# Attention values of a decoder block made in quarters between the conv blocks of the input projection

## The chip, the cores and the metric

The kernel runs on one core of one Trainium2 chip. The metric is the device time of one execution in microseconds; the time before is the median of 3 runs. The profile and its trace are of one further execution.

## The reference, cut to what matters

One layer of a hybrid decoder with 512 tokens of width 1024, in float32. Only the first half matters here:

```python
p = h @ W_in                      # columns: q | k | v | conv_B | conv_C | conv_u
q, k = rope(rmsnorm(q)), rope(rmsnorm(k))
o    = sliding_window_attention(q, k, v, sinks)   # window 128, blocks of 128 queries
conv = cb * short_conv(cc * cu, conv_w)           # width 3, causal
y    = concat([rmsnorm(o), rmsnorm(conv)]) @ W_out
x    = x + gate1 * y
```

The second half (a product-key expert layer over 16384 experts) takes most of the time and is the same before and after. In the attention a chunk of 128 queries has 8 heads; each head's scores against 128 or 256 keys get a mask, a maximum that takes in the sink, an exponential, a sum and a division, and the result multiplies the values.

## The kernel before, in words

Everything is laid out with features on the partitions and tokens along the free dimension. A product is three float32 matmuls with weights and activations split in a high and a low part: `parts` (line 184) loads 128x1024 weights into `raw`, ScalarE rounds them to `hi` (line 176), VectorE subtracts to `lo` (line 177), and `mm3` (line 197) issues 24 matmuls of 512 columns. `hi` and `lo` have 4 buffers each.

The first half is one Python loop over a string, `PLAN` (line 50), whose steps are written in the order in which their instructions are to be issued (loop from line 481). A step's letter says what it does:

- `Cmp`: conv block m, part p (`conv`, line 438): one `mm3` of 24 matmuls into a PSUM bank `pj`; part 0 is copied by ScalarE to `cc` (line 442), part 1 becomes the conv `y` on VectorE (lines 446 to 450), part 2 multiplies `y` into `convT` (line 452).
- `An`: scores of chunk n (`attend1`, line 374): 8 matmuls into four banks `sc`; VectorE takes them out into `s`, scaled and masked (line 388, 8 instructions), then the maximum (line 391) and its negative `nm` (line 394); ScalarE takes 8 exponentials (line 397) and a small one for the sink, `es_` (line 401); VectorE divides (line 405).
- `Bn`: values of chunk n (`attend2`, line 408): for each of 4 pairs of heads, TensorE transposes the probabilities into banks `pT` (line 416), ScalarE takes each head's bank out to `pT` in SBUF (line 418), and TensorE multiplies by the values into one bank `po` (line 425), one pair behind the transposes. ScalarE takes `po` out to `attnT` (line 434).
- `M`: two weight columns of the adaLN modulation as dot products on VectorE (`ada`, line 204, line 213); their DMA waits for the last `mm3` issued before.
- `S`, `N`: sums of squares of the conv output (line 236, matmul `ssc` line 237), and its RMSNorm (`part_norm`, line 463).

After the plan come the sums of squares of the attention output (`ssa`), and the output projection (`py`).

The Tile scheduler takes instructions in the order written as priority and settles, when the kernel is built, one fixed order for each engine; each engine then runs its instructions in that order and waits on semaphores. All of `sc`, `pT`, `po`, `pj` and the sums come from one pool of 6 PSUM banks (`bank`, line 110). In the plan before, the four steps `C30 C22 C31 C32` follow each other without attention work between them, and `B2` and `B3` stand behind them with only `S` and `N` between.

Of the kernel before, what the change touches and what calls it, by code (L numbers as in the profile page):

```python
# [19 lines left out]
T = 512  # L20
# [26 lines left out]

PLAN = ("q0 q1 k P2 M r0 V R P3 r1 q2 C00 r2 q3 T C01 M r3 M C02 A0 C10 M C11 A1 M C12 B0 C20 M M M A2 C21 B1 A3 "  # L50
        "C30 M C22 C31 C32 S B2 N B3 M M M")

SM = {}
_o = 0
# [35 lines left out]
def body(tc, p):  # L90
# [19 lines left out]
    def bank(name):  # L110
        return psm.tile([P, 512], F32, tag="m", name=name)
# [122 lines left out]
    def square(ps, b, i, n, w=None):  # L234
        q = tmp("sq")
        nc.scalar.activation(q, b, AF.Square)
        nc.tensor.matmul(ps, ones if w is None else w, q, start=(i == 0), stop=(i == n - 1))

    def rstd(ps, n):
        r = tmp("rstd")  # L240
        nc.scalar.activation(r, ps, AF.Sqrt, scale=1.0 / n, bias=eps)
        nc.vector.reciprocal(r, r)
        return r
# [10 lines left out]
    r1 = rstd(ps, D)  # L254
# [81 lines left out]
    def proj(b):  # L336
        w = weights_of(p["w_in"][b])
        ps = bank("pj")
        mm3(ps, w, hh, hlo)
        return ps  # L340

    def qk0(ps):
        ss = bank("ss")
        square(ss, ps, 0, 1, blk)
        return ss
# [4 lines left out]
    def q0(ps, b):  # L350

        qn = tmp("qn")
        nc.scalar.activation(qn, ps, AF.Identity, scale=S("qg"))
        q = tmp("sq")
        nc.scalar.activation(q, ps, AF.Square)
        for c in range(NCH):
            nc.tensor.matmul(ssq[:, c, b:b + 5:4], q[:, c * P:(c + 1) * P], blk[:, 0:65:64], start=True, stop=True)
        return qn

    def qk1(ps, ss, g):  # L360
        r = rstd(ss, 64)
        qn = tmp("qn")
        nc.vector.scalar_tensor_tensor(qn, ps, g, r, op0=OP.mult, op1=OP.mult)
        return qn

    def qk2(qn, dst):
        pr = bank("rot")
        nc.tensor.matmul(pr, perm, qn, start=True, stop=True)
        t2 = tmp("t2")
        nc.vector.tensor_mul(t2, pr, sinT)  # L370
        nc.vector.tensor_mul(qn, qn, cosT)
        nc.vector.tensor_add(dst, qn, t2)

    def attend1(n):
        k0 = 0 if n else P
        s = a1.tile([P, 8, 256], F32, tag="s", name="s", bufs=2)
        for b2 in range(2):
            pss = [bank("sc") for g in range(2)]
            for i in range(2):
                b = 2 * b2 + i  # L380
                for g, ps in enumerate(pss):
                    gp = slice(64 * g, 64 * g + 64)
                    nc.tensor.matmul(ps[:, i * 256 + k0:(i + 1) * 256], qT[gp, b, n * P:(n + 1) * P],
                                     kT[gp, (n - 1) * P + k0:(n + 1) * P], start=True, stop=True)
            for g, ps in enumerate(pss):
                for i in range(2):
                    h = 4 * g + 2 * b2 + i
                    nc.vector.scalar_tensor_tensor(s[:, h, k0:], ps[:, i * 256 + k0:(i + 1) * 256], rq[:, n, h:h + 1],
                                                   mask[:, k0:], op0=OP.mult, op1=OP.add)
        m = a1.tile([P, 8], F32, name="m", bufs=2)  # L390
        nc.vector.reduce_max(m, s[:, :, k0:], axis=X)
        nc.vector.tensor_max(m, m, S("sink"))
        nm = a1.tile([P, 8], F32, name="nm", bufs=2)
        nc.vector.tensor_scalar_mul(nm, m, -1.0)
        den = a1.tile([P, 8], F32, name="den", bufs=2)
        for h in range(8):
            nc.scalar.activation(s[:, h, k0:], s[:, h, k0:], AF.Exp, bias=nm[:, h:h + 1],
                                 accum_out=den[:, h:h + 1])
        es_ = a1.tile([P, 8], F32, name="es_", bufs=2)
        nc.vector.tensor_add(es_, S("sink"), nm)  # L400
        nc.scalar.activation(es_, es_, AF.Exp)
        nc.vector.tensor_add(den, den, es_)
        nc.vector.reciprocal(den, den)
        for h in range(8):
            nc.vector.tensor_scalar_mul(s[:, h, k0:], s[:, h, k0:], den[:, h:h + 1])
        return s

    def attend2(n, s):
        k0 = 0 if n else P
        po = bank("po")  # L410
        ptr, pT = {}, {}

        def turned(h):
            ptr = bank("pT")
            for kb in range(k0 // P, 2):
                nc.tensor.transpose(ptr[:, kb * P:(kb + 1) * P], s[:, h, kb * P:(kb + 1) * P], ident)
            pT[h] = a1.tile([P, 256], F32, tag="pT", name="pT", bufs=4)
            nc.scalar.activation(pT[h][:, k0:], ptr[:, k0:256], AF.Copy)

        def products(b):  # L420

            for kb in range(k0 // P, 2):
                for g in range(2):
                    gp = slice(64 * g, 64 * g + 64)
                    nc.tensor.matmul(po[gp, b * P:(b + 1) * P], vN[:, n - 1 + kb, gp],
                                     pT[b + 4 * g][:, kb * P:(kb + 1) * P], start=(kb == k0 // P), stop=(kb == 1))

        for b in range(4):
            turned(b)
            turned(b + 4)  # L430
            if b > 0:
                products(b - 1)
        products(3)
        nc.scalar.activation(attnT[:, :, n * P:(n + 1) * P], po.rearrange("p (a b) -> p a b", a=4), AF.Copy)

# [2 lines left out]
    def conv(m, part):  # L438
        ps = proj(6 + 3 * m + part)
        if part == 0:  # L440
            cv[m] = tmp("cc")
            nc.scalar.activation(cv[m], ps, AF.Copy)
        elif part == 1:
            hb = a1.tile([P, T + 2], F32, tag="hb", name="hb", bufs=1)
            nc.vector.memset(hb[:, 0:2], 0.0)
            nc.vector.tensor_mul(hb[:, 2:], ps, cv[m])
            y = cv[m] = tmp("y")
            nc.vector.tensor_scalar_mul(y, hb[:, 0:T], S("cw", m))
            for k in (1, 2):
                nc.vector.scalar_tensor_tensor(y, hb[:, k:k + T], S("cw", 4 * k + m), y, op0=OP.mult, op1=OP.add)  # L450
        else:
            nc.vector.tensor_mul(convT[:, m, :], ps, cv.pop(m))
# [3 lines left out]
    def more_ada(n=2):  # L456
        ada(rest[:n], mark[0])
        del rest[:n]
# [4 lines left out]
    def part_norm(ss, src, g, o):  # L463
        r = rstd(ss, 512)
        for k in range(4):
            f = tmp("f")
            nc.vector.scalar_tensor_tensor(f, src[:, k, :], S(g, k), r, op0=OP.mult, op1=OP.mult)
            split(mH[:, o + k, :], mL[:, o + k, :], f)
# [8 lines left out]
        mm3(py[b], wo[b], mh, ml, range(4 * half, 4 * half + 4))  # L477

    HEAD = 4
    sa, nq = {}, {}  # L480
    for step in PLAN.split():
        n = [int(x) for x in step[1:]]
        match step[0]:
            case "k":
                nk = qk1(pj[4], qk0(pj[4]), kg)
            case "q":
                nq[n[0]] = q0(pj[n[0]], n[0])
            case "P":
                pj[n[0]] = proj(n[0])
            case "V":  # L490
                pt = bank("vt")
                for c in range(NCH):
                    nc.tensor.transpose(pt[:, c * P:(c + 1) * P], vT[:, c * P:(c + 1) * P], ident)
                nc.scalar.activation(vN.rearrange("p a b -> p (a b)"), pt, AF.Copy)
            case "r":
                qk2(nq.pop(n[0]), qT[:, n[0], :])
            case "R":
                qk2(nk, kT)
            case "T":
                nc.scalar.activation(rq, ssq, AF.Sqrt, bias=eps64)  # L500
                nc.vector.reciprocal(rq, rq)
            case "A":
                sa[n[0]] = attend1(n[0])
            case "B":
                attend2(n[0], sa[n[0]])
            case "C":
                conv(*n)
            case "M":
                more_ada()
            case "S":  # L510
                ssc = bank("ssc")
                for k in range(4):
                    square(ssc, convT[:, k, :], k, 4)
            case "N":
                mH = a1.tile([P, DC, T], F32R, tag="hH", name="mH")
                mL = a1.tile([P, DC, T], F32R, tag="hL", name="mL")
                part_norm(ssc, convT, "cg", 0)
# [57 lines left out]
    r2 = rstd(ss2, D)  # L575
# [8 lines left out]
    for r, (dst, cs) in enumerate(((hN, slice(TD - P, TD)), (h2N, slice(TD, T)))):  # L584
        pg = [bank("pg0"), bank("pg1")]
        for k in range(DC):
            b = mod[:, 24 + k:25 + k]
# [551 lines left out]
```

## Time and profile before

| | |
|---|---|
| median of 3 runs | 1425.68 us (1423.78 to 1427.0) |
| profiled execution, its own time | 1432.56 us |
| its span | 1430.6 us |
| TensorE (PE) busy | 1391.4 us, 97% |
| VectorE (DVE) busy | 1227.8 us, 86% |
| ScalarE (ACT) busy | 616.8 us, 43% |
| stage of the plan that differs | from about 110 to about 190 us of the span |

Busy time on PE is the time in which a matmul is in its pipeline; ends are modelled, so overlapping neighbours show a duration longer than their spacing. A wait is given in brackets behind a row, with the instruction that ended it.

### The profile page before, as it was taken

The numbers are of one execution on the slowest core, as the hardware profiler recorded it, in microseconds if no ns is written. First come the engines' busy times: TensorE is split into PE (matmuls) and PEld (weight loads), VectorE is DVE, ScalarE is ACT, GpSimd is POOL, SyncE is SP. The second block draws the span as 40 slices with busy tenths as digits, with TensorE's granted clock in tenths as the row PEclk, the third lists the DMA queues.
The fourth block names the chain that finished last, engine by engine and source line by source line (L and its number), as shares of the span: only waits on it lengthen the run. The fifth ranks groups of instructions, "written<-read, shape, count | busy, mean of one in ns | idle before, by whom it ended". The sixth has DMA issues, their size and how long they took to land.

```text
span 1430.6 us, 21234 instructions
## 1 busy us (share of the span) xinstructions
PE 1391.4 (97%) x7696; PEld 1220.9 (85%) x7696; DVE 1227.8 (86%) x2251; ACT 616.8 (43%) x1041; POOL 441.1 (31%) x308
## 2 busy tenths in 40 slices
PE   6999998999999999999999999999999999999998
PEld 4676776888999999999888888889888999998896
DVE  7778978689999998978995888878787899997896
ACT  4524645534745545554343433433334433333332
POOL 0000001332023410003112434446664566645540
PEclk9999999999999999999999999999999999999999
DMA  7645536232598987789989999999999899999984
GB/s 270 226 156 187 195 123 202 89 98 80 177 325 293 395 339 280 297 306 347 365 300 327 348 360 386 375 366 337 347 382 358 330 403 396 405 360 352 356 324 147
DMA packets 134376, 418.80 MB, mean 293 GB/s; under 512 B 12800, under 2 KB 39552, under 8 KB 132736
## 3 DMA queue, kind: packets, MB, share of 16 engines
q1 hardware_dynamic: 92800, 266.45, 51.5%
q0 software_dynamic: 41472, 151.01, 28.0%
q8 instruction: 60, 0.98, 0.3%
q14 instruction: 44, 0.36, 0.1%
HBM read 375.77 MB, written 41.62 MB: 292 GB/s over the span
## 4 chain that ended last, share of the span: by engine, by line
PE 42%; issue 11%; DVE 10%; DMA 7%; POOL 6%; ACT 0%; DVEq 0%; POOLq 0%; ACTq 0%
PE pa L200 7%; PE pa L202 7%; PE pa L201 7%; PE o L1005 6%; PE o L1004 6%; PE o L1003 6%; POOL row L776 5%; DMA row<-in_uR,eG 5%; DVE ga L919 3%; DVE lo L177 2%; DMA row<-in_vL,eG 2%; PE gps L961 2%; PE gps L962 1%; DVE junk L784 1%; DVE wwl L177 1%
## 5 line engine op out<-in xcount | busy, mean ns | idle before, releaser
L176 ACT ACTIVATE hi<-raw 128x1024 fp32r<-128x1024 f32 x298 | 312.6, 1054 | 331.2 <-issue 121.7
L177 DVE TENSOR_TENSOR lo<-raw,hi 128x1024 fp32r<-128x1024 f32 x282 | 343.8, 1220 | 21.9 <-ACT hi L176 21.3
L202 PE MATMUL pa<-h2H,lo 128*128 128x352 f32 x1024 | 331.7, 324 | 5.3 <-DVE lo L177 5.2
L200 PE MATMUL pa<-h2H,hi 128*128 128x352 f32 x1024 | 333.0, 325 | 0.0
L201 PE MATMUL pa<-h2L,hi 128*128 128x352 f32 x1024 | 329.8, 322 | 0.0
L1004 PE MATMUL o<-lo,wwh 128*128 128x512 f32 x768 | 299.5, 390 | 1.4 <-DVE lo L177 1.4
L1005 PE MATMUL o<-hi,wwl 128*128 128x512 f32 x768 | 299.3, 390 | 0.9 <-DVE wwl L177 0.9
L1003 PE MATMUL o<-hi,wwh 128*128 128x512 f32 x768 | 299.6, 390 | 0.0
L776 POOL DMA_INDIRECT row<-in_uR,eG x128 | 179.6, 1403 | 383.6 <-PE o L1005 179.8
L776 POOL DMA_INDIRECT row<-in_vL,eG x128 | 176.4, 1378 | 131.8 <-DVE ga L919 58.4
L784 DVE SCALAR_TENSOR_TENSOR junk<-row,h2N 128x1024 bf16<-128x1024 f32 x128 | 154.0, 1221 | 69.8 <-DMA row<-in_uR,eG 69.8
L202 PEld LDWEIGHTS pa<-h2H,lo 128*128 128x128 f32 x1024 | 193.7, 189 | 7.5 <-DVE lo L177 7.5
L201 PEld LDWEIGHTS pa<-h2L,hi 128*128 128x128 f32 x1024 | 193.2, 189 | 2.2
L200 PEld LDWEIGHTS pa<-h2H,hi 128*128 128x128 f32 x1024 | 192.8, 188 | 2.2
L919 DVE SCALAR_TENSOR_TENSOR ga<-row,av,ga 128x1024 f32<-128x1024 f32 x127 | 163.2, 1285 | 18.4 <-DMA row<-in_vL,eG 13.7
L1005 PEld LDWEIGHTS o<-hi,wwl 128*128 128x128 f32 x768 | 144.2, 188 | 32.4 <-DVE wwl L177 2.4
L1004 PEld LDWEIGHTS o<-lo,wwh 128*128 128x128 f32 x768 | 144.1, 188 | 31.1 <-DVE lo L177 2.9
L1003 PEld LDWEIGHTS o<-hi,wwh 128*128 128x128 f32 x768 | 144.1, 188 | 28.0 <-issue 0.2
L177 POOL TENSOR_TENSOR lo<-raw,hi 128x1024 fp32r<-128x1024 f32 x16 | 39.1, 2447 | 298.7 <-ACT hi L176 296.4
L176 ACT ACTIVATE wwh<-w 128x768 fp32r<-128x768 f32 x64 | 53.9, 843 | 165.0 <-DVE w L986 122.6
L985 ACT ACTIVATE w<-G 128x32 f32<-128x32 f32 x128 | 22.2, 221 | 175.8 <-DVE wwl L177 174.3
L776 POOL DMA_INDIRECT row<-in_uR,eH x32 | 45.7, 1427 | 130.1 <-DVE junk L784 72.3
(266 smaller groups left out, 1899.0 us busy)
## 6 DMA issues: line engine op xcount, KB each, us to landing
raw<-in_uL SPq DMA_DIRECT2D x128, 512.0 KB
raw<-in_vL SPq DMA_DIRECT2D x128, 512.0 KB
Gd<-st SPq DMA_DIRECT2D x12, 2048.0 KB
G<-Gd SPq DMA_DIRECT2D x16, 1536.0 KB
ada<-in_ada SPq DMA_DIRECT2D x32, 512.0 KB
Ad<-sp SPq DMA_DIRECT2D x34, 352.0 KB
sp<-Ad SPq DMA_DIRECT2D x34, 352.0 KB
raw<-in_w_in SPq DMA_DIRECT2D x18, 512.0 KB
```

The lines of the kernel that those rows point to most:

```text
L176: nc.scalar.activation(h, f, AF.Copy)
L177: by.tensor_sub(l, f, h.bitcast(F32))
L200: nc.tensor.matmul(ps, wh(k), rh(k), start=(k == k0), stop=False)
L201: nc.tensor.matmul(ps, wh(k), rl(k), start=False, stop=False)
L202: mark[0] = nc.tensor.matmul(ps, wl(k), rh(k), start=False, stop=(k == k1))
L776: d = nc.gpsimd.indirect_dma_start(out=t, out_offset=None, in_=tab, in_offset=bass.IndirectOffsetOnAxis(ap=e, axis=0))
L784: return nc.vector.scalar_tensor_tensor(junk, t, 1.0, h, op0=OP.mult, op1=OP.mult, accum_out=a)
L919: nc.vector.scalar_tensor_tensor(ga, t, av[:, k:k + 1], ga, op0=OP.mult, op1=OP.add)
L961: nc.tensor.matmul(o, A[:, 4 * b + t], B1[:, 4 * b + t], start=True, stop=False)
L1003: nc.tensor.matmul(o, wh[:, cs], vh[:, hs], start=(j == 0), stop=False)
L1004: nc.tensor.matmul(o, wh[:, cs], vl[:, hs], start=False, stop=False)
L1005: last = nc.tensor.matmul(o, wl[:, cs], vh[:, hs], start=False, stop=(j == NJ - 1))
```

## The change

`attend2` becomes a generator that stops after each of its first three pairs of heads, so that a step `Bn` makes one quarter; each chunk's `B` now stands four times in the plan. The plan's order changes as well: `C20` goes ahead of the first `B0`; two quarters each of chunks 0, 1 and 2 follow a conv block; the scores `A2` and `A3` move behind the last quarter of `B0` and `B1`, that is later than before; the dots `M` move with them; the last two quarters of `B2` stand behind `S`, and all of `B3` behind `N`. No instruction is added or taken away.

```diff
-PLAN = ("q0 q1 k P2 M r0 V R P3 r1 q2 C00 r2 q3 T C01 M r3 M C02 A0 C10 M C11 A1 M C12 B0 C20 M M M A2 C21 B1 A3 "
-        "C30 M C22 C31 C32 S B2 N B3 M M M")
+PLAN = ("q0 q1 k P2 M r0 V R P3 r1 q2 C00 r2 q3 T C01 M r3 M C02 A0 C10 M C11 A1 M C12 C20 B0 B0 M M M C21 B0 B0 A2 "
+        "C30 B1 B1 M C22 B1 B1 A3 C31 B2 B2 C32 S B2 B2 N B3 B3 B3 B3 M M M")
...
             turned(b + 4)
             if b > 0:
                 products(b - 1)
+            if b < 3:
+                yield
         products(3)
...
-    sa, nq = {}, {}
+    sa, nq, values = {}, {}, {}
...
             case "B":
-                attend2(n[0], sa[n[0]])
+                if n[0] not in values:
+                    values[n[0]] = attend2(n[0], sa[n[0]])
+                next(values[n[0]], None)
```

TensorE at chunk 0's values, before (the first row is the last matmul of `C12`, the last the first of `C20`):

```order
L202 MATMUL pj<-hH,lo 128x512
L416 MATMUL pT<-cst,s 128x128 x4
L425 MATMUL po<-pT,vN 64x128 x2
L416 MATMUL pT<-cst,s 128x128 x2
L425 MATMUL po<-pT,vN 64x128 x2
L416 MATMUL pT<-cst,s 128x128 x2
L425 MATMUL po<-pT,vN 64x128 x4
L200 MATMUL pj<-hH,hi 128x512
```

Now (the first row is the last matmul of `C20`, the last the first of `C21`):

```order
L202 MATMUL pj<-hH,lo 128x512
L416 MATMUL pT<-cst,s 128x128 x4
L425 MATMUL po<-pT,vN 64x128 x2
L200 MATMUL pj<-hH,hi 128x512
```

`C20` has moved ahead of the first transposes, and only the first half of the values stands between it and `C21`; its other half stands behind `C21`.

ScalarE from the small exponential of chunk 0 to the evictions of chunk 0's values, before (`s_846` and `nm_870` are chunk 1's scores and maximum, `cc_1007` the copy of `C20`, `pT_937` the first eviction of chunk 0):

```order
L401 ACTIVATE es__754<-es__754 128x8
L176 ACTIVATE hi_1227<-raw_1225 128x1024
L176 ACTIVATE hi_1268<-raw_1266 128x1024
L418 ACTIVATE pT_937<-pT_935 128x128
L418 ACTIVATE pT_941<-pT_939 128x128
L418 ACTIVATE pT_945<-pT_943 128x128
L418 ACTIVATE pT_949<-pT_947 128x128
L418 ACTIVATE pT_955<-pT_953 128x128
L418 ACTIVATE pT_959<-pT_957 128x128
L418 ACTIVATE pT_965<-pT_963 128x128
L418 ACTIVATE pT_969<-pT_967 128x128
L434 ACTIVATE attnT_446<-po_934 128x4x128
```

Now (`cc_965` is the copy of `C20`; `pT_970` and the three after it are chunk 0's first half, `pT_1050` begins its second, `hi_1363` holds the weights of `C32`):

```order
L401 ACTIVATE es__754<-es__754 128x8
L176 ACTIVATE hi_1121<-raw_1119 128x1024
L176 ACTIVATE hi_1187<-raw_1185 128x1024
L176 ACTIVATE hi_1300<-raw_1298 128x1024
L397 ACTIVATE s_846,den_872<-s_846,nm_870 128x256 x8
L401 ACTIVATE es__881<-es__881 128x8
L444 ACTIVATE cc_965<-pj_940 128x512
L418 ACTIVATE pT_970<-pT_968 128x128
L418 ACTIVATE pT_974<-pT_972 128x128
L418 ACTIVATE pT_978<-pT_976 128x128
L418 ACTIVATE pT_982<-pT_980 128x128
L176 ACTIVATE hi_1363<-raw_1361 128x1024
```

Before, all evictions of chunk 0 stood ahead of chunk 1's exponentials. Now chunk 1's exponentials and the copy of `C20` stand ahead of them.

ScalarE around chunk 3's exponentials, now (`attnT<-po` is chunk 1's, the second `s,den` chunk 3's, the `pT` behind it chunk 2's first half):

```order
L436 ACTIVATE attnT<-po 128x4x128
L397 ACTIVATE s,den<-s,nm 128x256 x8
L401 ACTIVATE es__1285<-es__1285 128x8
L418 ACTIVATE pT<-pT 128x256 x4
L236 ACTIVATE sq<-convT 128x512 x3
L176 ACTIVATE hi<-raw 128x1024 x2
L236 ACTIVATE sq<-convT 128x512
```

Chunk 2's first half has moved from behind all the conv blocks to a place between `C31` and `C32`, and its evictions stand directly behind chunk 3's exponentials.

## Rows read from the trace of the kernel before

**Rows 1.** The page: busy time of each engine.

```profile
PE 1391.4 (97%) x7696; PEld 1220.9 (85%) x7696; DVE 1227.8 (86%) x2251; ACT 616.8 (43%) x1041; POOL 441.1 (31%) x308
```

**Rows 2.** Stretches: us, busy of PE, PEld, DVE, ACT, POOL, granted clock, DMA share, GB/s.

```profile
118.00:126.00 8.00, 7.13 (x30) 4.50 (x31) 8.00 (x16) 3.34 (x12) 0.00 (x0) 0.57 0.00 0
182.00:190.00 8.00, 6.49 (x14) 3.40 (x15) 5.33 (x10) 4.34 (x8) 0.00 (x0) 0.79 0.20 72
```

**Rows 3.** Timeline of PE, 115 to 185: start, duration, instruction [idle before <-releaser].

```profile
115.46 0.33 PE L416 MATMUL pT<-cst,s 128*128 128x128 f32 x1
117.23 0.33 PE L416 MATMUL pT<-cst,s 128*128 128x128 f32 x1 [1.44 <-DVE s L388]
...
119.67 0.69 PE L425 MATMUL po<-pT,vN 128*64 128x128 f32 x4 [0.40 <-ACT pT L418]
...
123.27 0.80 PE L200 MATMUL pj<-hH,hi 128*128 128x512 f32 x1
...
129.89 2.00 PE L383 MATMUL sc<-kT,qT 64*128 64x256 f32 x16
131.82 0.50 PE L200 MATMUL pj<-hH,hi 128*128 128x512 f32 x1
137.44 1.09 PE L416 MATMUL pT<-cst,s 128*128 128x128 f32 x8
138.97 0.40 PE L425 MATMUL po<-pT,vN 128*64 128x128 f32 x2 [0.44 <-DVE s L388]
...
143.03 2.00 PE L383 MATMUL sc<-kT,qT 64*128 64x256 f32 x16
144.96 0.50 PE L200 MATMUL pj<-hH,hi 128*128 128x512 f32 x1
...
166.85 2.74 PE L237 MATMUL ssc<-sq,ones 128*128 128x512 f32 x6
...
179.96 1.31 PE L425 MATMUL po<-pT,vN 128*64 128x128 f32 x16
183.51 2.08 PE L237 MATMUL ssa<-sq,ones 128*128 128x512 f32 x2 [2.24 <-ACT sq L236]
```

**Rows 4.** Timeline of DVE, chunk 1's scores.

```profile
116.69 2.83 DVE L388 SCALAR_TENSOR_TENSOR s<-sc,rq,cs 128x256 f32<-128x256 f32 x7
...
120.58 2.29 DVE L391 TENSOR_REDUCE m<-s 128x8 f32<-128x2048 f32 x1
...
124.59 0.17 DVE L394 TENSOR_SCALAR nm<-m 128x8 f32<-128x8 f32 x1
```

**Rows 5.** Timeline of ACT, from chunk 1's exponentials to the first evictions of its values.

```profile
124.80 0.51 ACT L397 ACTIVATE s<-s,nm 128x256 f32<-128x256 f32 x1 [0.82 <-DVE hb L445]
...
128.76 0.19 ACT L401 ACTIVATE es__881<-es__881 128x8 f32<-128x8 f32 x1
130.00 0.60 ACT L442 ACTIVATE cc<-pj 128x512 f32<-128x512 f32 x1 [1.05 <-PE pj L202]
...
137.41 1.06 ACT L176 ACTIVATE hi<-raw 128x1024 fp32r<-128x1024 f32 x1 [5.86 <-PE pj L201]
138.37 1.19 ACT L418 ACTIVATE pT<-pT 128x256 f32<-128x256 f32 x4
```

**Rows 6.** Stretches of 1 us, columns as in rows 2: where the granted clock changes.

```profile
118.00:119.00 1.00, 0.53 (x2) 0.32 (x2) 1.00 (x3) 0.28 (x1) 0.00 (x0) 0.73 0.00 0
...
125.00:126.00 1.00, 1.00 (x5) 0.76 (x5) 1.00 (x3) 1.00 (x5) 0.00 (x0) 0.85 0.00 0
...
183.00:184.00 1.00, 0.49 (x1) 0.49 (x2) 1.00 (x3) 0.98 (x2) 0.00 (x0) 0.66 0.00 0
...
186.00:187.00 1.00, 1.00 (x3) 0.42 (x2) 1.00 (x2) 0.12 (x1) 0.00 (x0) 0.63 0.45 115
```

**Rows 7.** Waits, 188 to 300: engine line <- releaser: total us, times, longest.

```profile
DVE xT L544 <- PE py L202: 4.0, 3, 2.6
```

**Rows 8.** A stretch of the expert layer, columns as in rows 2.

```profile
400.00:450.00 50.00, 50.00 (x339) 49.71 (x338) 49.23 (x75) 21.35 (x37) 11.75 (x10) 1.00 0.88 298
```

## The prediction

> **What bounds the kernel now.** I read the page first: PE is busy 97% of the span [rows 1], and in the expert layer it never stops, 50.00 us of 50 [rows 8]. So the end is set by PE's in-order work, and what PE loses anywhere ahead of the expert layer arrives at the end one for one, unless a later wait is set by something that does not move with it. The one candidate I looked for lies behind the attention, where VectorE waits for PE's output projection 4.0 us in 3 waits [rows 7]: there too the waiting goes by PE, so a delay passes through.
>
> Then I took the stretch that the change touches. In the stretches of 8 us, PE is busy 7.13 us at a mean clock of 0.57 from 118 to 126, and 6.49 us at 0.79 from 182 to 190 [rows 2]. The timeline of PE says why: after `C12`'s last matmul chunk 0's transposes wait for VectorE to take chunk 1's scores out of their banks (1.44 us and two like it), and at the end the sums `ssa` wait 2.24 us for ScalarE [rows 3]. Rows of 1 us show the clock at 1.2 instead of 2.4 GHz from about 118.5 to 125.3 and from about 183.3 to 186.6 [rows 6]. The conv blocks from 144.96 to 166.85 run without a gap: 21.89 us for four, 5.47 each [rows 3].
>
> **What the change takes away.** From `C12`'s end (115.46) to `C21`'s end (137.44) PE took 21.98 us for two conv blocks (10.94), chunk 2's scores (131.82 - 129.89 = 1.93) and chunk 0's values. Those have no undisturbed row of their own; chunk 1's, with twice the keys, took 143.03 - 137.44 = 5.59 less 0.44 idle, and half of that is 2.58 [rows 3]. The rest, 21.98 - 10.94 - 1.93 - 2.58 = **6.5 us**, is waiting for banks and half clock. With `C20` put ahead of chunk 0's values the scores of chunk 1 are out of their banks at 116.69 + 2.83 = 119.5 [rows 4], before `C20` ends at 115.46 + 5.47 = 120.9. The bank wait goes, all of the 6.5 us.
>
> **What it puts in its place.** The first half of chunk 0's values now needs ScalarE's evictions, and these stand behind chunk 1's exponentials and the copy of `C20` in ScalarE's order. Nothing that the exponentials wait for is earlier than before: VectorE's maximum of chunk 1 is a 2.29 us reduction at 120.58 behind the scores, and its negative is written at 124.59 to 124.8 [rows 4]. VectorE's order is unchanged up to there, and it was busy all of the 8 us from 118 to 126 [rows 2], so this time holds. The exponentials run from 124.80 to the small one's end, 128.76 + 0.19 = 128.95 [rows 5]. Then the copy (0.60) and the first two evictions (1.19 / 4 = 0.30 each) [rows 5]: the products can go at 129.9 and 130.1. PE has its four transposes done at 121.3 and stands 8.6 us. Each engine runs in its own order, so nothing behind these products, `C21` first, can go before.
>
> The clock: after a gap of 2.24 us it was low for 3.1 us of dense work (183.51 to 186.6), after the scattered waits for 5.6 us (119.67 to 125.3) [rows 3, 6]. Half of that is lost: 1.6 to 2.8 us; I take 2.2. `C21` runs 130.3 to 138.0.
>
> The second half of chunk 0: its four evictions stand behind a rounding of weights (1.06) that waits for the conv block's end, as the row at 137.41 did [rows 5]; four evictions end at 140.2, the last products at 140.4, and 7 of 8 score matmuls of chunk 2 (1.7) follow: **142.1**, where the kernel before stood at 137.44. The changed order is 4.7 us behind, gain and loss together.
>
> From there to the end of chunk 3's scores both do `C30`, `C22`, chunk 1's values and the scores: 2 x 5.47 + 5.59 + 1.93 = 18.46, to 160.6. Cutting chunk 1's values in two costs nothing by this: each half has evictions behind a rounding, as the whole has now. Bounds: -0.4 (today's 0.44 us wait gone) to +1.5 (a rounding and a half in front of each half). I take 0.
>
> Then the same loss again. `C31` ends at 166.0, the eight transposes of chunk 2's first half at 167.1 (1.09). Their evictions stand behind chunk 3's exponentials. These need 8 extractions (2.83 / 7 = 0.40 each, from 159.6 when the first bank is full: 162.8), the reduction (2.2: 165.0), the small steps (0.3), and 128.95 - 124.80 = 4.15 for the exponentials: 169.5, and two evictions: 170.1. PE stands **3.0 us**. Before, four conv blocks stood behind chunk 3's scores and covered this chain of some 9 us; now one does. Bounds: 2 (VectorE gets there quicker) to 4.5 (a dot of 1.2 us in between). The clock then falls as after the 2.24 us gap: 1.6; bounds 0 (it doesn't) and 2.8.
>
> The tail, from the end of `C32` (166.85) to the last product (179.96 + 1.31 = 181.27), only loses the 1.75 us of chunk 2 that were done earlier, which is no gain; I allow 0.6 for a wait there that closes. The dots `M` and their DMAs move on VectorE and SP, but no row has PE waiting for them; 0. The 2.24 us before `ssa` stay: last eviction, square and sum stand in the same order.
>
> **Sum:** 4.7 + 0 + 3.0 + 1.6 - 0.6 = **+8.7 us**. The profiled execution took 1432.56 us, 6.9 above the median of the runs; against it the sum gives 1441.3, against the median of 1425.68 it gives **1434.4**.
>
> **A rule against this reading.** The Trainium skill, Perfetto Trace Analysis, Optimization Strategy, says that repeated gaps on the engine that should be full can mean that there is too little SBUF or PSUM for the next tile. The 1.44 us row agrees: the releaser is VectorE's extraction from a bank. By that rule alone the sum would be -6.5 us, 1419.2; it is the first rival.
>
> **The rivals.**
> - *Banks only: faster, 1419 to 1422.* The bank wait goes and the evictions are no later than PE wants them. For it: 6.5 us lie there, and the conv block placed in front outlasts the extractions by 1.4 us. It decides by when chunk 1's exponentials end: the sum up to chunk 2's scores is even if they end 4.7 us earlier, at 124.2, and that is before they begin now. It would take evictions that pass waiting exponentials on ScalarE. The trace has them in issue order everywhere: the eviction at 138.37 sat behind a rounding that waited for PE [rows 5]. TensorE: Matmul & The Clock Gate in the Trainium skill, on the array's architecture, calls ScalarE's queue strictly first in, first out; the trace agrees with the row at 138.37. 0.08.
> - *No difference, 1424 to 1428.* The delay is real and is taken back behind the attention, by the gap before `ssa` or at the output projection. Against it: those waits name PE or hang on PE's last product [rows 3, 7]. Or chunk 3's chain is covered and the clock recovers at once: that leaves 4.7 - 0.6 = 4.1, still slower. 0.10.
> - *Worse, 1437 to 1440.* Both clock falls last 5.6 us (+0.6 and +1.2), chunk 1's halves wait (+1.5), a dot gets between (+1.5): +13.5 at most. 0.15.
>
> **How the numbers follow.** My own case, 1429 to 1437, has 0.67. What a measurement of this kernel can tell is about 0.2%, 2.9 us. Low end of my case: 8.7 - 0.6 - 1.6 - 1.0 - 0.4 = +5.1, or 1430.8, less 1.5 for the spread of the runs. Range: 1428 to 1440, which takes in most of the worse case and the edge of no difference. Faster 0.08, same 0.10, slower 0.82.
>
> **What would show it.** Right: PE idle some 8 us between `C20` and `C21` with ScalarE's evictions (line 418) as releaser, instead of line 388; a clock of 0.5 when `C21` begins; a second gap of about 3 us between `C31` and `C32`; `ssa` some 8 to 9 us later than 183.51. Wrong in the first step: `C21` starts before 128. Wrong in the second: no gap before `C32`. Wrong in the passing on: `ssa` late by this much and the end not.

## The result and the profile after

The changed kernel took **1438.76 us**, median of 6 runs (1436.91 to 1441.04), the kernel before beside it 1426.34 us, median of 6 (1423.78 to 1430.3). The ratio is 1.0079, 95% interval 1.0062 to 1.0095, or 11.3 us (8.8 to 13.5) slower. Measured once more later, the same kernel gave 1.0072 (1.0052 to 1.0091). The profiled execution took 1441.04 us with a span of 1439.1.

The page of the changed kernel, busy time of each engine, against [rows 1]:

```profile
PE 1391.1 (97%) x7696; PEld 1220.9 (85%) x7696; DVE 1231.5 (86%) x2251; ACT 615.9 (43%) x1041; POOL 441.1 (31%) x308
```

PE's 1391 us are the same as before, so what was added to the span is time in which PE is idle. The stretches of the changed kernel, columns as in [rows 2]:

```profile
118.00:126.00 8.00, 2.58 (x14) 1.94 (x12) 8.00 (x15) 2.98 (x9) 0.00 (x0) 0.89 0.41 127
126.00:134.00 8.00, 5.09 (x14) 3.89 (x15) 7.25 (x18) 3.34 (x16) 0.00 (x0) 0.50 0.85 269
```

Where PE was busy 7.13 us of 8 before, it is now busy 2.58; in the next stretch it is idle for 2.91 us and at half clock throughout. VectorE is busy all of the first and 7.25 us of the second. The timeline of PE of the changed kernel, to be held against [rows 3]:

```profile
119.99 0.60 PE L416 MATMUL pT<-cst,s 128*128 128x128 f32 x4
128.91 0.85 PE L425 MATMUL po<-pT,vN 128*64 128x128 f32 x4 [8.33 <-ACT pT L418]
129.69 0.79 PE L200 MATMUL pj<-hH,hi 128*128 128x512 f32 x1
...
137.55 0.38 PE L416 MATMUL pT<-cst,s 128*128 128x128 f32 x2
...
149.17 0.43 PE L425 MATMUL po<-pT,vN 128*64 128x128 f32 x2 [0.81 <-ACT pT L418]
...
166.33 1.03 PE L416 MATMUL pT<-cst,s 128*128 128x128 f32 x8
170.44 0.43 PE L425 MATMUL po<-pT,vN 128*64 128x128 f32 x2 [3.07 <-ACT pT L418]
...
178.76 3.60 PE L237 MATMUL ssc<-sq,ones 128*128 128x512 f32 x8
...
193.37 6.67 PE L237 MATMUL ssa<-sq,ones 128*128 128x512 f32 x8 [2.76 <-ACT sq L236]
```

The releaser `DVE s L388` of [rows 3] is gone at chunk 0's values. In its place PE stands 8.33 us after the first four transposes and 3.07 us after the eight of chunk 2, both times for ScalarE's evictions of the transposed probabilities (line 418). `C21` takes 7.86 us (129.69 to 137.55) instead of 5.47. What VectorE and ScalarE did in those 8.33 us:

```profile
123.29 0.67 DVE L454 TENSOR_TENSOR convT<-pj,y 128x512 f32<-128x512 f32 x1
123.89 0.15 DVE L394 TENSOR_SCALAR nm<-m 128x8 f32<-128x8 f32 x1
```

```profile
124.08 0.51 ACT L397 ACTIVATE s<-s,nm 128x256 f32<-128x256 f32 x1 [3.02 <-DVE hb L447]
...
128.03 0.19 ACT L401 ACTIVATE es__881<-es__881 128x8 f32<-128x8 f32 x1
128.13 0.57 ACT L444 ACTIVATE cc<-pj 128x512 f32<-128x512 f32 x1
128.61 0.74 ACT L418 ACTIVATE pT<-pT 128x128 f32<-128x128 f32 x4
```

ScalarE itself was idle for the 3.02 us ahead of the first exponential: the evictions stood ready behind exponentials that could not start before VectorE had the negated maximum `nm` (123.89 + 0.15 = 124.04; the row names `hb`, a memset that ended at the same time). It is the chain of [rows 4, 5], some 0.7 us earlier in the span, with the evictions now behind it. As before the change, two dots of 1.2 us each stand in that chain on VectorE, at 118.73 ahead of the maximum and at 122.07 behind it; the changed kernel with these two moved and nothing else was not tried.

### The profile page after: what moved, and what is told of

The parts are those of the page before. It is cut to its first block, busy times and chain, and to the rows that moved or that the text cites. A ratio compares the mean times of both kernels' runs of the same rounds, so it can differ in the third digit from the quotient of the medians.

```text
span 1439.1 us, 21234 instructions
## 1 busy us (share of the span) xinstructions
PE 1391.1 (97%) x7696; PEld 1220.9 (85%) x7696; DVE 1231.5 (86%) x2251; ACT 615.9 (43%) x1041; POOL 441.1 (31%) x308
## 4 chain that ended last, share of the span: by engine, by line
PE 48%; DVE 11%; issue 10%; DMA 4%; POOL 3%; ACT 0%; DVEq 0%; POOLq 0%
PE o L1008 8%; PE o L1009 8%; PE o L1007 8%; PE pa L200 7%; PE pa L202 7%; PE pa L201 7%; DVE ga L923 4%; POOL row L780 3%; DMA row<-in_uR,eG 2%; DVE lo L177 2%; DMA row<-in_vL,eG 2%; PE gps L965 2%; PE gps L966 1%; DVE junk L788 1%; DVE wwl L177 1%
## 5 line engine op out<-in xcount | busy, mean ns | idle before, releaser
L176 ACT ACTIVATE wwh<-w 128x768 fp32r<-128x768 f32 x64 | 54.0, 843 | 165.2 <-DVE w L990 128.9
L780 POOL DMA_INDIRECT row<-in_uR,eH x32 | 45.8, 1430 | 129.2 <-DVE junk L788 76.1
```

The source lines that it names most:

```text
L176: nc.scalar.activation(h, f, AF.Copy)
L780: d = nc.gpsimd.indirect_dma_start(out=t, out_offset=None, in_=tab, in_offset=bass.IndirectOffsetOnAxis(ap=e, axis=0))
```

## The experiments

Several versions are compared by a count within the trace, since the time at which this stage begins scatters from run to run (118.0 to 122.9 us of the span): from `C20`'s end (the first transposes of chunk 0; in the order of before, `C12`'s end plus the 5.47 us of one conv block) to the first `ssa`, and to the first scores `psc` of the expert layer. Each count is that of one traced execution. Two numbers are two traces of the same order. "Wait 1" is PE's at chunk 0's values, "wait 2" the one ahead of `C32`.

| version | wait 1, us | wait 2, us | to `ssa`, us | to `psc`, us | ratio to before (95%) |
|---|---|---|---|---|---|
| before | banks | none | 62.58, 62.77 | 136.99, 136.11 | 1.0003 (0.9983 to 1.0023) |
| changed | 8.33, 7.83 | 3.07, 3.07 | 73.38, 71.98 | 148.34, 145.45 | 1.0079, 1.0072 |
| `C20` first only | 7.69 | none | 66.44 | 141.53 | 1.0021 (1.0002 to 1.0041) |
| changed, chunk 1's exponentials behind | 2.82 | 1.60 | 70.99 | 145.09 | 1.0063 (1.0039 to 1.0087) |
| changed, chunk 3's exponentials behind | 7.82 | 1.01 | 69.46 | 143.95 | 1.0058 (1.0034 to 1.0081) |
| changed, wait 1 filled | 0.28 | 4.40 | 75.18 | 148.69 | 1.0102 (1.0067 to 1.0136) |
| changed, both behind | 2.43, 2.75 | none | 65.39, 70.48 | 138.63, 144.00 | 1.0051 (1.0030 to 1.0073), 1.0064 (1.0042 to 1.0086) |
| both behind, dots moved | 1.18 | none | 74.73 | 151.82 | 1.0092 (1.0072 to 1.0112) |
| `C20` first, chunk 1's exponentials behind | 2.04 | none | 61.53 | 136.47 | 1.0013 (0.9990 to 1.0036) |
| the same, 2 dots moved | 1.18 | none | 60.53 | 136.08 | 0.9989 (0.9968 to 1.0009) |
| the same, 6 dots moved | 1.18 | none | 59.26 | 135.76 | 0.9998 (0.9981 to 1.0015) |

My theory: the evictions wait behind chunk 1's and chunk 3's exponentials in ScalarE's order, and the clock falls in these waits. Rivals: the cut (a bank held through two conv blocks), and the moved dots, scores and transfers.

**`C20` first and nothing else.** On the kernel before:

```diff
-... A1 M C12 B0 C20 M M M A2 C21 B1 A3 ...
+... A1 M C12 C20 B0 M M M A2 C21 B1 A3 ...
```

> The kernel before with C20 put ahead of chunk 0's values and nothing else: the values are whole, no step is cut, no dot or score moves. In ScalarE's order chunk 1's exponentials and the copy of C20 now stand ahead of chunk 0's evictions, as in the changed kernel. My theory (the evictions wait behind the exponentials): the bank waits go (-6.5 us), PE stands about 8 us at chunk 0's values with ScalarE's evictions as releaser, the clock costs about 2.4 behind it, and no second wait before C32: +4 against the kernel before, 1428 to 1433 us. Rival 1 (the bank rule: the waits for banks were the cost, and cutting the values in quarters, which holds a bank through two conv blocks, is what costs now): no cut here, so -6.5, about 1420. Rival 2 (the moved dots, scores and transfers cost): they do not move here, so about -6.5 as well.

Measured: 1431.27 us, ratio 1.0021. The timeline of PE in this version:

```profile
119.44 0.60 PE L416 MATMUL pT<-cst,s 128*128 128x128 f32 x4
127.72 0.85 PE L425 MATMUL po<-pT,vN 128*64 128x128 f32 x4 [7.69 <-ACT pT L418]
...
131.48 3.77 PE L383 MATMUL sc<-kT,qT 64*128 64x256 f32 x16
```

The wait is there without any cut and with every dot where it was; chunk 2's scores run at half clock (3.77 us instead of 2.00 [rows 3]). Both rivals asked for 1420 and fall. This one move makes the kernel slower by some 3 us by the ratio (0.3 to 5.9), where 4 were expected; by the count it is 3.8 us late at `ssa` and 5.0 at `psc`, where the changed kernel is 10.0 and 10.3 late (means of the two traces).

**Chunk 1's exponentials behind the evictions.** `attend1` ends after `nm`; the exponentials and the division become a step `E`, which stands directly behind `A` except where shown:

```diff
         nc.vector.tensor_scalar_mul(nm, m, -1.0)
+        return s, nm
+
+    def softmax(n, s, nm):
+        k0 = 0 if n else P
...
-... C12 C20 B0 B0 M M M C21 ...
+... C12 C20 B0 B0 E1 M M M C21 ...
```

> The changed kernel with one thing more: chunk 1's exponentials and division are issued behind the first half of chunk 0's values, so that four of chunk 0's evictions stand ahead of them on ScalarE. My theory: the wait of 8.3 us between C20 and C21 goes to under 1 us and the 2.4 us of low clock in C21 with it, while the wait of 3.1 us before C32 stays: 10 us less than the changed kernel, 1427 to 1431 us. Rivals (banks held through conv blocks, the cut, moved dots and transfers): the order of the plan and the cut are as in the changed kernel, so 1437 to 1441.

Measured: 1437.79 us, ratio 1.0063: at most some 2 us better than the changed kernel, not 10. By the time alone the rivals' band (1437 to 1441) came true; what moving the exponentials did is read from the trace. The waits of PE in this version, 100 to 300 us (lines are 4 further down: 420 for 416, 422 for 418, 429 for 425, 458 for 454):

```profile
PE po L429 <- DVE hb L451: 2.8, 1, 2.8
...
PE po L429 <- ACT pT L422: 2.2, 3, 1.6
PE po L429 <- DVE s L388: 1.4, 1, 1.4
PE sc L383 <- DVE s L388: 1.0, 1, 1.0
PE pT L420 <- ACT cc L448: 0.8, 1, 0.8
```

The exponentials are out of the way, `C21` runs at full clock (125.38 to 130.97), and a second wait shows that lay under the first: 2.82 us with VectorE as releaser. Then three more, 1.4, 1.0 and 0.8 us, at chunk 1's values and chunk 3's scores. Up to `C21`'s end this version is 8.2 us ahead of the changed kernel; it loses most of that between there and `C31`. Chunk 1's second half and chunk 3's scores alone take 10.1 us (151.36 to 161.43) instead of 4.9, with two waits in them and the granted clock at 0.50 from 158 to 161. Wait 2, for its part, was 1.60 us instead of the 3.1 expected: chunk 3's scores came in pieces, VectorE had half of them out before the last piece ran, and was done with them 1.0 us behind PE instead of 2.5. What VectorE did when the first wait ended:

```profile
124.19 0.68 DVE L458 TENSOR_TENSOR convT<-pj,y 128x512 f32<-128x512 f32 x1
...
124.89 0.06 DVE L451 MEMSET hb<- 128x2 f32 x1
```

PE's products start at 125.01. The instruction named writes only SBUF; the multiplication of `C12` just ahead of it reads a bank `pj` until 124.87, and the products need a bank for `po`. The version with moved dots, below, tests that.

**Chunk 3's exponentials behind the evictions.**

```diff
-... A3 C31 B2 B2 C32 ...
+... A3 C31 B2 B2 E3 C32 ...
```

> The changed kernel with chunk 3's exponentials issued behind the first half of chunk 2's values; in ScalarE's order four of the eight now stand behind that half's evictions. My theory: the wait before C32 falls from 3.1 us by four exponentials of 0.5 us to about 1.0, and the clock behind it costs 0 to 1.9 us less: 2 to 4 us less than the changed kernel, 1435 to 1437 us, with the first wait of 8.3 us unchanged. If the second wait is taken back later in the tail, which waits for ScalarE at the sums of the attention output anyway, the time stays at 1438 to 1440.

Measured: wait 2 is 1.01 us, as expected, and wait 1 is still 7.82. The time, 1436.46 us (1.0058), lies 2 to 3 us under the changed kernel's, but the intervals overlap; that the evictions' place sets wait 2 rests on the trace.

**Wait 1 filled.** In `attend2`, behind the second pair of transposes of chunk 0, and held behind the last of them:

```diff
+            if n == 0 and b == 1:
+                fill = psa.tile([P, 512], F32, tag="a", name="fill")
+                for i in range(34):
+                    after(nc.tensor.matmul(fill, hh(i % 8)[:, 0:P], hh(i % 8), start=(i == 0), stop=(i == 33)), last[0])
             if b > 0:
                 products(b - 1)
```

> The changed kernel with 34 matmuls of 512 columns into a spare bank, whose result nobody reads, between chunk 0's first transposes and the products that wait for ScalarE: about 34 x 0.23 = 7.7 us of the 8.3 us wait are filled, so the wait's end stays where it was and PE's clock does not fall in it. My theory (the low clock behind the wait costs 2.4 us in C21): C21 takes 5.5 us instead of 7.9, and the kernel 2 to 2.5 us less than the changed one, 1436 to 1437 us. If the clock's fall costs nothing at the end (given back later), 1438 to 1440; if the added matmuls themselves run at half clock they outlast the wait by some 6 us, 1443 or more.

Measured: 1443.13 us, ratio 1.0102, not faster than the changed kernel; by the medians it is slower, with intervals that overlap. Its timeline of PE:

```profile
121.93 7.98 PE L434 MATMUL fill<-hH 128*128 128x512 f32 x34
130.18 0.59 PE L425 MATMUL po<-pT,vN 128*64 128x128 f32 x4 [0.28 <-ACT pT L418]
130.71 0.50 PE L200 MATMUL pj<-hH,hi 128*128 128x512 f32 x1
...
138.73 0.70 PE L383 MATMUL sc<-kT,qT 64*128 64x256 f32 x2 [1.33 <-DVE hb L452]
...
172.80 0.69 PE L425 MATMUL po<-pT,vN 128*64 128x128 f32 x2 [4.40 <-ACT pT L418]
```

The step itself went as expected: the clock stayed at 1.00 and `C21` took 5.58 us (130.71 to 136.29) instead of 7.86. But then PE waits 1.33 us for VectorE ahead of chunk 2's scores, and wait 2 grows from 3.07 to 4.40. VectorE's `nm` of chunk 3 stands at 168.13, 46.6 us behind `C20`'s end; in the changed kernel it stood at 165.77, 45.8 behind. PE came earlier and VectorE did not: in the 40 us from `C20`'s end VectorE stands 6.8 us for the transfers of its dots, in the changed kernel 1.9 and 1.0 in the two traces. Why the transfers came later is open. The low clock was not removed either but moved: at wait 2 it was 0.50 from 172 to 178.7, in the changed kernel for some 3.4 us in either trace. None of my three branches came out: the time lies in the band of the third (1443 or more), but the added matmuls ran at full clock, 34 in 7.98 us; that the clock's fall costs nothing at the end asked for 1438 to 1440. To `psc` this trace is 1.8 us behind the mean of the changed kernel's two (148.69 against 146.9), by the ratios it is some 3 to 4 us; the rest stays open.

**Both pairs of evictions ahead.** `E1` and `E3` moved as above.

> The changed kernel with both pairs of evictions put ahead of the exponentials that delayed them: chunk 1's exponentials behind chunk 0's first half and chunk 3's behind chunk 2's. If the two edits add up: moving chunk 1's alone brought the start of the output projection 4.0 us earlier against the first transposes of chunk 0 (199.48 - 119.99 = 79.49 in the changed kernel, 75.53 there), moving chunk 3's alone 5.3 us, so both leave 12.2 - 9.3 = 3 us against the kernel before: 1429 to 1431 us. If chunk 3's wait hangs on VectorE, which is late by then (chunk 1's divisions come later), the second edit gives less here: 1433 to 1437.

Measured: 1435.9 us, ratio 1.0051, above the sum of the two and in the band of the other branch, though chunk 3's wait was gone. The trace of that run, the fastest of its 6 executions, stood only 2 us above before. So it ran once more:

> The changed kernel with both pairs of evictions ahead of the exponentials, once more, since its stage and its time disagreed: in its trace the first scores of the expert layer started 1.6 us later than in the kernel before, counted from the end of C20, but its median stood 7.8 us above the median of before. If the profile of that run was a lucky one, this trace shows a first wait or a second one that is longer, and 5 to 8 us at that place; if the difference arises behind it, 1.6 us there again and a median of 1433 to 1437; if the median was the chance, 1428 to 1432.

Measured: 1438.87 us, ratio 1.0064, and 144.00 to `psc`, 5.4 us more than the first trace, with nearly the same waits (2.75 and 2.43; 0.97 and 0.45 in both). The difference arises ahead of `ssa` (5.1 us), and it is the clock. Behind the first wait `C21` took 8.28 us (126.62 to 134.90) against 6.69 (123.51 to 130.20) in the first trace. The larger part comes later. Stretches of 1 us of the second trace, columns as in [rows 2]:

```profile
159.00:160.00 1.00, 0.69 (x3) 0.52 (x4) 0.96 (x4) 1.00 (x4) 0.00 (x0) 0.84 0.11 29
160.00:161.00 1.00, 1.00 (x4) 0.35 (x5) 0.96 (x5) 0.06 (x1) 0.00 (x0) 0.50 0.00 0
...
165.00:166.00 1.00, 1.00 (x3) 0.81 (x3) 0.97 (x3) 0.00 (x0) 0.00 (x0) 0.50 0.00 0
166.00:167.00 1.00, 1.00 (x4) 0.77 (x4) 1.00 (x1) 0.00 (x0) 0.00 (x0) 0.75 0.00 0
```

The first trace, at the same place (2.8 us earlier in its span), has no such fall:

```profile
157.00:158.00 1.00, 1.00 (x7) 0.61 (x4) 1.00 (x5) 0.32 (x1) 0.00 (x0) 1.00 0.00 0
...
162.00:163.00 1.00, 1.00 (x6) 0.83 (x5) 0.11 (x1) 1.00 (x5) 0.00 (x0) 1.00 0.00 0
```

The profile of the first run was a lucky one, as the first branch of the expectation had it, though not by its waits. The order set the waits to within 0.4 us in the two traces; whether the clock fell behind a row of short ones differed.

**The dots of `C12` moved to the plan's end.** On the version with both pairs ahead:

```diff
-... A1 M C12 C20 ... B3 M M M
+... A1 C12 C20 ... B3 M M M M
```

> The same as the kernel with both pairs of evictions ahead, and the two dots between A1 and C12 moved to the plan's end. In VectorE's order the multiplication into convT of C12 then stands directly behind chunk 1's scores, some 4 us earlier, and frees the bank that chunk 0's products take. Theory 1 (a bank held by that multiplication is what remains of the first wait, 2.82 us, once the exponentials are out of the way): the wait falls to some 1.2 us, given by ScalarE's rounding and copy (1.06 + 0.58), less the 0.35 of the transposes; 1.5 us less than the kernel without the dots moved, and more where VectorE, two dots lighter, is the later one at chunk 1's and 2's waits: 1426 to 1429. Theory 2 (only ScalarE's order matters): no difference beyond 0.2%.

Measured: wait 1 fell from 2.43 to 1.18 us with ScalarE as releaser, since `C12`'s multiplication now ran at 117.39, counted from `C20`'s end some 4 us earlier: a bank had been the second wait. But the time rose to 1440.83 us (1.0092, with an interval that reaches into that of the version without the dots moved); the trace is of the slowest of the 6 executions. VectorE and PE in this version:

```profile
117.39 0.69 DVE L458 TENSOR_TENSOR convT<-pj,y 128x512 f32<-128x512 f32 x1
```

```profile
121.03 0.60 PE L429 MATMUL po<-pT,vN 128*64 128x128 f32 x4 [1.18 <-ACT pT L422]
...
139.35 0.44 PE L420 MATMUL pT<-cst,s 128*128 128x128 f32 x2 [1.51 <-DVE s L388]
143.22 1.47 PE L420 MATMUL pT<-cst,s 128*128 128x128 f32 x4 [3.43 <-DVE s L388]
```

```profile
DVE junk L213 <- DMA ada<-in_ada: 10.5, 6, 4.1
```

VectorE stands 10.5 us at six dots for their transfers, from 100 to 192 us (7.1 and 5.5 in the two traces of the version without the dots moved). Each transfer is held behind the last `mm3` issued ahead of it, and with two dots fewer on the way VectorE comes to the next ones, which stand in its order ahead of chunk 2's scores, before their data is there: one waits 4.1 us. PE then waits 4.9 us for the banks of these scores, and behind that the granted clock is 0.50 from 142 to 148 and again from 159 to 168. Both theories missed the sign, and this reading of VectorE's rows was not tested by itself.

**On the plan of before.** `C20` first, whole values, and chunk 1's exponentials behind them; then with the two dots of `C12` moved to the end; then with four more dots moved behind `S` and `B2`:

```diff
-... A1 M C12 B0 C20 M M M A2 C21 B1 A3 C30 M C22 C31 C32 S B2 N B3 M M M
+... A1 M C12 C20 B0 E1 M M M A2 C21 B1 A3 C30 M C22 C31 C32 S B2 N B3 M M M
...
+... A1 C12 C20 B0 E1 M M M A2 C21 B1 A3 C30 M C22 C31 C32 S B2 N B3 M M M M
...
+... A1 C12 C20 B0 E1 M A2 C21 B1 A3 C30 M C22 C31 C32 S M B2 M N B3 M M M M
```

> The kernel before with C20 ahead of chunk 0's whole values and chunk 1's exponentials and division issued behind them; no cut in quarters. My theory: of the 7.69 us wait that C20 first alone left, some 2.8 stay (the bank that VectorE's multiplication into convT holds), and the 2 us of low clock behind it go; chunk 1's later division gives some 2 us back at chunk 1's values. Against C20 first alone -5 to -7, so at or a little below the kernel before: 1422 to 1427 us. If VectorE bounds this stretch, the wait only moves to chunk 1's values and chunk 2's scores: 1428 to 1432.

> The same with the two dots between A1 and C12 moved to the plan's end, so that the bank of C12 is freed some 4 us earlier. My theory: the first wait falls to some 1.2 us, and VectorE is 2.4 us less loaded up to chunk 3's scores: 1.5 to 3 us less than without the dots moved, 1420 to 1425 us, a version that beats both kernels if it falls below 1423. If only ScalarE's order matters: as without the dots moved.

> The version with C20 and whole values ahead of chunk 1's exponentials and the two dots of C12 moved, and with four more dots moved: of the three steps M behind chunk 0's values two now stand behind S and behind chunk 2's values, where VectorE is busy 57 to 79% instead of 90 to 100. My theory (once ScalarE's order is mended, VectorE is the bound from 110 to 170): the wait of 1.89 us at chunk 1's values, whose releaser is the extraction of chunk 2's scores, goes, and the low clock behind it (mean 0.85 from 140 to 150, 1.5 us) with it: 3 us less than that version, 1421 to 1425 us on the same scale as 1427 for the kernel before. If VectorE is no bound: as that version, 1425 to 1428.

Measured: 1431.11 us (1.0013), 1426.28 (0.9989) and 1428.67 (0.9998): none differs measurably from the kernel before, and all three lie above what my theory asked for, the first where I had put it if VectorE bounds this stretch. The waits for chunk 1's scores at chunk 0's transposes are gone in all three, and in the last the 1.89 us at chunk 1's values as well. A low clock is not gone: it was at 0.50 from 124 to 130 in the first, from 140 to 142 in the second and from 123 to 126 in the third. The count shows where the last version's gain went. To `ssa` the last version is 3.4 us ahead of before; to `psc` 0.8. Behind the output projection PE now waits:

```profile
PE ss L557 <- DVE sq L223: 2.9, 1, 2.9
```

Before, that place had 0.65 us with ScalarE as releaser. The dots that left the stage are done on VectorE behind it, and PE finds VectorE late there. A later wait, ahead of the matmuls `pq`, is 1.3 us shorter, so PE stands only some 1.1 us longer from `ssa` to `psc`; the rest of the 2.6 us given back is time in which PE is busy, part of it at low clock behind that wait (0.50 from 229 to 232). No version beat both kernels.

**The two kernels again.**

> The changed kernel itself, for a second trace and for times beside the version with both edits. My theory: waits of 8 and 3 us at the two places again, within 0.3 us, since both hang on orders fixed when the kernel is built; 10 to 13 us above the kernel before. If the two waits were chance, they differ by more than 1 us.

> The kernel before, unchanged, for a second trace: in the first the execution took 6.9 us more than the median of the runs. Counted from C12's end plus one conv block (5.47) the first scores of the expert layer stood 136.99 us later there; over all the versions measured so far the differences between medians lie some 2 us above the differences by this count. If the first trace of before was a slow one in this stage (its clock low for longer than usual), this trace shows 133 to 136. If the count is right, it is 137 again, and the 2 us arise elsewhere. The time itself: 1.000 times the kernel before, within 0.2%.

Measured: the changed kernel 1439.7 us, waits of 7.83 and 3.07 (the first 0.5 less than in the first trace, more than the 0.3 that I allowed and less than the 1 of chance); the kernel before 1.0003 of itself, 136.11 to `psc`, 0.9 less than in its first trace, all of it behind `ssa`. That is only part of the 2 us by which the medians' differences exceed the count's; the rest stays open. By the two pairs of traces the change costs 10.3 us to `psc` (146.9 less 136.55), near the 11.3 of the ratio. Up to `ssa`, from one conv block ahead of `C20`'s end, PE is idle for 15.0 and 14.5 us in the changed kernel and for 6.0 and 5.9 before: 8.9 and 8.6 of the 10.8 and 9.2 us that are lost there are idle time.

## Why the prediction was right, and where it was short

- *The bank wait goes, all of the 6.5 us:* right at the place where it was seen; line 388 no longer releases PE there. Not right as a gain to be had: under the new wait lies another bank, held by `C12`'s multiplication (2.82 us, shown by moving the dots), and where both are cleared, on the plan of before, the gain up to `ssa` (2.2 and 3.4 us) is mostly taken back behind it.
- *PE stands 8.6 us between `C20` and `C21`:* 8.33 and 7.83, by the chain that was named. `C20` put first alone reproduces it.
- *Clock loss 2.2:* 2.4 (7.86 less 5.47) and 1.5 (7.01 less 5.47) in the two traces. Filling the wait removed it at this place, which shows the cause; that it is worth 2.2 us at the end is not shown, since in that version wait 2 and the low clock behind it grew.
- *4.7 us behind at the end of chunk 2's scores:* 5.2 (21.74 against 16.51) and 3.7 (20.39 against 16.74).
- *Cutting chunk 1's values costs 0:* 0.6 (141.73 to 160.75 is 19.02, against 18.46; 19.03 in the second trace), most of it from the wait of 0.81 where before had 0.44. Within the bounds, but the term was mis-sized.
- *Second wait 3.0:* 3.07 in both traces. Its clock loss 1.6: 1.9 (170.44 to 178.76 is 8.32; at full clock, with both pairs ahead, the same work took 164.22 to 170.64, 6.42).
- *The tail, -0.6 beyond the 1.75 moved:* -0.8 (`ssc` to the last product 11.85 against 14.42).
- *The 2.24 us before `ssa` stay:* they became 2.76 in both traces. This step failed; 0.5.
- *The dots move at no cost:* no row of the changed kernel has PE waiting for a dot, as predicted. But they are not free: VectorE waits for their transfers in its own order, and with two of them moved PE waited 4.9 us in one version, by a reading that was not tested by itself.

Up to `ssa` the two pairs give +10.8 and +9.2 against the forecast's +8.7; the terms mis-sized are chunk 1's halves (0.6), the second clock loss (0.3) and the wait before `ssa` (0.5); the first clock loss came out above its 2.2 in one trace and below it in the other, so that its fit is in part luck. The sum came out just under the interval of 8.8 to 13.5; the median of 1438.76 lies 4.4 above the forecast, inside the range, but above the 1429 to 1437 of my own case. It falls into the band of the rival "worse" (1437 to 1440), of whose mechanisms two came in part: the low clock behind the first wait lasted 5.6 us in the first trace (128.9 to 134.5) and 3.9 in the second, and chunk 1's halves waited. No dot got between in chunk 3's chain. The rival "banks only" is refuted by the result and by the first experiment. The Trainium skill (Perfetto Trace Analysis, Optimization Strategy) says that the same gap, repeating on the engine that should be full, can mean too little SBUF or PSUM for the next tile. The traces agree for two waits for a bank, 1.44 us before the change and 2.82 us under the 8.33; in the changed kernel the wait that ended last there was ScalarE's.

*The passing on:* a loss on PE went through to the end, as the prediction said. Its converse, that what PE gains arrives as well, was not claimed there but stood in my expectations for nearly every experiment, and it did not hold here: VectorE is busy 88 to 100% in five of the six stretches of 10 us from 110 to 170 of the kernel before (72% in the one from 120), and what PE gained there was lost again, in part at waits with VectorE as releaser (1.4 and 1.0 us with chunk 1's exponentials behind, 2.9 with six dots moved) and in part by the low clock behind such waits. A count of waits on the bounding engine alone does not show this; it needs the second engine's rows in the same stretch, its busy share and what it waits for in its own order. How much of each loss is VectorE's work and how much the transfers of its dots was not separated.

## What to carry to other kernels

When work is put earlier on the bounding engine, look in the order of every engine that serves it for what now stands ahead of its service, and date that by the chain that releases it: here evictions of 0.3 us stood behind exponentials that started 3.5 us after the evictions could have. A wait that is removed shows the one beneath it, so price a removal by the next wait to end, not by the whole of the one that is seen. Where a second engine is nearly full over the stretch, do not count on a gain on the first to arrive: here the loss passed through to the end, and the gains of up to 3.4 us did not.

## What the runs showed of the hardware

PE's granted clock fell to 0.50 (1.2 GHz) while PE stood in the 8 us wait, in both traces of the changed kernel, and was back at 1.00 about half-way through `C21` (134.5 and 133.5). In the first trace:

```profile
123.00:124.00 1.00, 0.00 (x0) 0.00 (x0) 1.00 (x7) 0.00 (x0) 0.00 (x0) 1.00 0.04 16
124.00:125.00 1.00, 0.00 (x0) 0.00 (x0) 1.00 (x3) 0.92 (x4) 0.00 (x0) 0.65 0.64 127
...
134.00:135.00 1.00, 1.00 (x4) 0.74 (x4) 0.26 (x2) 0.00 (x0) 0.00 (x0) 0.73 0.79 315
135.00:136.00 1.00, 1.00 (x6) 0.81 (x5) 0.78 (x1) 0.00 (x0) 0.00 (x0) 1.00 0.88 324
```

With matmuls in the wait it did not leave 1.00 there:

```profile
128.00:129.00 1.00, 1.00 (x6) 0.84 (x5) 1.00 (x2) 1.00 (x5) 0.00 (x0) 1.00 0.94 332
```

Yet the same order of instructions, with waits of 8.33 and 7.83 us, lost 2.4 us in one execution and 1.5 in the other. Ahead of `C32` the fall came only after PE had resumed at 170.44, between 172 and 173 (in the second trace between 171 and 172):

```profile
170.00:171.00 1.00, 0.56 (x3) 0.38 (x3) 0.78 (x4) 1.00 (x6) 0.00 (x0) 1.00 0.00 0
171.00:172.00 1.00, 1.00 (x8) 0.60 (x8) 1.00 (x5) 1.00 (x3) 0.00 (x0) 1.00 0.00 0
172.00:173.00 1.00, 1.00 (x3) 0.77 (x3) 0.78 (x3) 1.00 (x3) 0.00 (x0) 0.54 0.00 0
173.00:174.00 1.00, 1.00 (x4) 0.74 (x3) 0.27 (x1) 0.70 (x1) 0.00 (x0) 0.50 0.00 0
```

So a gap's price in clock is not paid in the gap, and one trace does not tell it: with both pairs of evictions ahead, two executions of one program differed by 5.1 us up to `ssa`, nearly all of it time at low clock.
